# Low parts of weight sums by accumulating transfers in place of VectorE subtractions

## The chip, the cores and the metric

The kernel runs on one core of a Trainium2 chip. The core has a matrix engine (TensorE, PE in the profile), VectorE (DVE), ScalarE (ACT), GpSimd (POOL) and SyncE (SP), each with its own queue of instructions that it works off in order, and 16 DMA engines that all queues share. TensorE writes to PSUM banks; the others work on SBUF tiles of 128 partitions. The metric is the device time of one execution in microseconds.

## The reference, cut to what matters

The reference is one layer of a hybrid block on 256 tokens of width 2048: a gated delta rule branch and a sparse attention branch, merged and projected, then a layer norm, a gated feed-forward part of hidden width 5632, and a second layer norm. All of it is float32. What matters here is the first half of the feed-forward part:

```python
h_gate, h_up = jnp.split(x @ w_ffn_in[l], 2, axis=-1)
x = layer_norm(DEEPNORM_ALPHA * x + (jax.nn.silu(h_gate) * h_up) @ w_ffn_out[l], ln2_g[l], ln2_b[l])
```

## The kernel before

**Split numbers.** TensorE multiplies in a rounded form of float32 (fp32r). To keep precision, each operand is split into a high part (the rounded value, by a ScalarE copy) and a low part (the value minus the high part, by a VectorE subtraction), and a product is three matmuls: high by high, low by high, high by low (`mm3`, L217 to L219). `split(hi, lo, src)` at L207 to L209 is one such copy and one such subtraction.

**Chunks.** Weights stream in chunks of 128 partitions by 1024 numbers (512 KB). `chunk` (L84 to L94) issues the load on SyncE's queue into one of four `raw` tiles, the copy to `hi` on ScalarE (L91) and the subtraction to `lo` on VectorE (L93).

**Groups.** The first feed-forward product runs as a first block, `wfi`, in two parts, and then ten groups (`x_group`, i = 1 to 10), each with 1024 columns of `wfg` and eight pairs of chunks. Some pairs of a group take seven products in place of eight, by Strassen's scheme (`seven_pair`): they need sums of the weight tiles (t1 to t4), split into high and low parts, beside forms of the activations (`f_form`). Their partial results go to four PSUM banks that are read by `sums_chain` (L1065 to L1072). Each group takes four banks (`aux` or `acc`) for its result and four of the other kind for these partial results, and the kinds swap from group to group, so a group's first matmuls write banks that `sums_chain` of the group before must have read. Group 1 runs pairs 0 to 7 in order, with seven products in pairs 4 and 6. Groups 2 and 3 run pairs 1, 3, 2, 0, 4, 5, 6, 7, with seven products in 0, 2, 4 and 6.

**Ready sums.** In most pairs the sums are made in `seven_pair` itself. For pair 0 of groups 2 and 3 (`NEAR`) they are made ahead, in `f_forms_chain`, while group 1 runs, and kept in `near` tiles. `near[0]` is one pair of raw tiles that serves both groups one after the other; `near[1]` and `near[2]` hold the high and low parts for group 2, `near[3]` and `near[4]` those for group 3. For each group the chain issues two loads (L1390, SyncE), makes four sums in place in the raw tiles (`four_sums`, VectorE, L934, L935, L938, L939) and splits the two tiles (L208 on ScalarE, L209 on VectorE).

**Order.** The program is written as a main line with side chains. The main line calls `tick()` after each half pair; `yield n` in a chain means "go on n ticks later". TensorE's and SyncE's queues hold their instructions in the order in which the code issues them (`manual_schedule`). The order on ScalarE, VectorE and GpSimd is made by a planner that goes by readiness in its own model and by priority; loads and splits of chunks have a priority some 70 instructions ahead of their place. Counted from the start of group 1 (16 ticks per group), the chain's loads for group 2 stand at ticks 3 and 4, the sums at 6 and 7, the splits at 8 and 9; the loads for group 3 at 13 and 14, the sums at 16 and 17, the splits at 18 and 19. `sums_of` then hands the tiles to `seven_pair` (L269), which reads them as t1 to t4 in the fourth pair of groups 2 and 3.

**GpSimd's queue** in this stretch holds stores of hidden rows to memory (`put_out`, L1250) and of their forms (L1462).

Of the kernel before, what the change touches and what calls it, by code (L numbers as in the profile page):

```python
# [8 lines left out]
F32 = mybir.dt.float32  # L9
F32R = mybir.dt.float32r  # L10
U32 = mybir.dt.uint32
AF = mybir.ActivationFunctionType
OP = mybir.AluOpType
# [50 lines left out]
def block_kernel(ctx: ExitStack, tc: tile.TileContext, xT, x, cpack, onehot, relb, convw, alog, dtb, gnw,  # L64
                 ws, wws, win, wz, wgt, wba, wbb, woa, wob, wfi, wfg, wfo, ln1g, ln1b, ln2g, ln2b, out):
    nc = tc.nc
# [17 lines left out]
    def chunk(src, pool=None, lead=LEAD):  # L84
        n = src.shape[1]
        pool = pool or wp
        with tc.high_priority(offset=lead):
            raw = wp.tile([P, n], F32, name="raw", tag="raw")
            nc.sync.dma_start(raw, src)
            hi = pool.tile([P, n], F32R, name="hi", tag="hi")  # L90
            nc.scalar.copy(hi, raw)  # L91
            lo = pool.tile([P, n], F32R, name="lo", tag="lo")
            nc.vector.tensor_sub(lo, raw, hi.bitcast(F32))  # L93
        return hi, lo  # L94
# [112 lines left out]
    def split(hi, lo, src):  # L207
        nc.scalar.copy(hi, src)  # L208
        nc.vector.tensor_sub(lo, src, hi.bitcast(F32))  # L209
# [225 lines left out]
    for i in range(8):  # L435
        k0 = 2 * i
        parts = [srcs[i]] if i > 2 else [srcs[i][:, :512], srcs[i][:, 512:]]
        for j, src in enumerate(parts):
# [9 lines left out]
            else:  # L448
                split(*xp, xr)
                hi, lo = chunk(src, lead=0)  # L450
# [479 lines left out]
    def four_sums(ra, rb, lead=0):  # L930

        r0, r1, s0, s1 = (t[:, n * 512:n * 512 + 512] for t in (ra, rb) for n in range(2))
        with tc.high_priority(offset=lead):
            nc.vector.tensor_add(r0, r0, s1)  # L934
            nc.vector.tensor_add(s1, r1, s1)  # L935
        yield 1
        with tc.high_priority(offset=lead):
            nc.vector.tensor_add(r1, r0, r1)  # L938
            nc.vector.tensor_add(s0, r1, s0)  # L939
# [113 lines left out]
    def x_form(q, dst, x32, g):  # L1053
        x32 = x32.rearrange("p (k t) -> p k t", k=2)
        g = g.rearrange("p (i t) -> p i t", i=4)
        ks = slice(2 * q % 4, 2 * q % 4 + 2)
        nc.vector.tensor_add(x32, XH[q // 2][:, ks].bitcast(F32), XL[q // 2][:, ks].bitcast(F32))
        forms([g[:, j] for j in range(4)], x32[:, 0, :P], x32[:, 0, P:], x32[:, 1, :P], x32[:, 1, P:])
        split(*dst, g)
# [192 lines left out]
    def fetch(i, j):  # L1252
# [4 lines left out]
    near = [[hp_.tile([P, 1024], F32R if i > 1 else F32, name="near", tag=f"{hl}{i}") for hl in ("hH", "hL")]  # L1257
            for i in range(1, 5)]
# [74 lines left out]
    def fv():  # L1333
        return fp.tile([P, 512], F32, name="v", tag="v", bufs=4)
# [41 lines left out]
    def f_forms_chain():  # L1376
        yield "x1"
        for tb in range(NTB):
            yield 2
            nc.sync.dma_start(d_x1[tb], x1[tb])  # L1380
        t = [rp.tile([P, 2, 2, 4, P], F32R, name="f_form", tag=f"x1_{tb}") for tb in range(NTB)]
        for i, q in enumerate((4, 6, 2, 0)):
            yield 1
            f_form[q] = t[i // 2][:, i % 2, 0], t[i // 2][:, i % 2, 1]
            x_form(q, f_form[q], fv(), fv())
        yield 1
        raw = near[0]
        for m, g in enumerate(NEAR):
            for i in range(2):
                nc.sync.dma_start(raw[i], wfg[g - 1, i])  # L1390
                yield 1
            yield 1
            yield from four_sums(*raw)
            for i in range(2):
                yield 1
                split(near[1 + 2 * m][i], near[2 + 2 * m][i], raw[i])
            k_ready[g][0] = sums_of(near[1 + 2 * m], near[2 + 2 * m])
            yield 4

    k_ready = {g: {} for g in KEPT + NEAR}  # L1400

    def sums_of(hi, lo):
        (t1, t2), (t4, t3) = ([(hi[i][:, n * 512:n * 512 + 512], lo[i][:, n * 512:n * 512 + 512]) for n in range(2)]
                              for i in range(2))
        return t1, t2, t3, t4

    def kept_load(m):
# [8 lines left out]
        k_ready[KEPT[m]][0] = sums_of(*zip(*kept))  # L1416

    start(f_forms_chain())
    for tb, ps in enumerate(block_xs([wfi[1, k] for k in range(8)], xh, xl)):
        start(h_chain(1, tb, gated(tb, ps), ps_acc))  # L1420
# [325 lines left out]
```

## Time and profile before

| | |
|---|---|
| median of 3 runs | 1456.29 us (1454.67 to 1456.54) |
| the profiled execution's own time | 1454.49 us |
| its span, first to last instruction | 1452.7 us |
| granted TensorE clock | 0.999 |
| group 1's matmuls | about 794 to 836 us of the span |

All times in profile rows count from the start of the span. A row of a timeline gives the start, the duration in us, the engine, the line, the operation with output and input tiles, and in brackets the idle time of the engine just before with what ended it. A row of busy time by stage gives the stretch and its length, then the busy us and the number of instructions of TensorE, its weight loads, VectorE, ScalarE and GpSimd, then the granted clock, the busy share of the 16 DMA engines and GB/s. A row of a tile's view gives the least, median and greatest duration in ns and the first and last start; its last line gives the time from a transfer's issue to its landing. A row of a queue gives packets, MB and its share of the 16 engines' time.

### The profile page before, as it was taken

How to read it: one execution, taken by the hardware profiler on the slowest of the kernel's cores; microseconds unless marked ns; L12 is line 12 of the kernel's file. 1: busy time of each engine (PE TensorE's matmuls, PEld its weight loads, DVE VectorE, ACT ScalarE, POOL GpSimd, SP SyncE). 2: the span in 40 equal slices, each digit the busy share in tenths (PEclk: the TensorE clock that was granted, in tenths of full speed). 3: DMA queues.
4: the chain of work that ended last, by engine and by line, in shares of the span. 5: the costliest groups of instructions: out<-in, count | busy, mean ns of one | idle time of the engine just before them, and what ended most of it. 6: DMA issues, size and time to landing. Idle time of an engine off the chain costs nothing.

```text
span 1452.7 us, 19640 instructions
## 1 busy us (share of the span) xinstructions
PE 1443.7 (99%) x7140; PEld 1213.8 (84%) x7140; DVE 1279.0 (88%) x1763; ACT 813.9 (56%) x1021; POOL 56.2 (4%) x75
## 2 busy tenths in 40 slices
PE   9999999999999999999999999999999999999998
PEld 8888888888888888888888878888888888888887
DVE  6798988789699959998886999989999998989987
ACT  5765454557456646655435665656566565554552
POOL 0002011121000000000000000000000000000000
PEclk9999999999999999999999999999999999999999
DMA  8646589854556755756856767777766666887863
GB/s 293 197 159 196 175 216 335 295 187 151 169 198 232 233 193 198 247 188 204 304 202 218 264 236 253 251 271 255 279 211 212 216 215 247 311 342 265 315 215 118
DMA packets 101969, 336.40 MB, mean 232 GB/s; under 512 B 17696, under 2 KB 18888, under 8 KB 101360
## 3 DMA queue, kind: packets, MB, share of 16 engines
q1 hardware_dynamic: 88512, 310.03, 62.0%
q0 software_dynamic: 6176, 22.75, 4.6%
q10 hardware_dynamic: 7184, 2.36, 0.7%
q8 instruction: 56, 0.92, 0.2%
q14 instruction: 41, 0.34, 0.1%
HBM read 312.88 MB, written 22.22 MB: 231 GB/s over the span
## 4 chain that ended last, share of the span: by engine, by line
PE 92%; DVE 3%; DMA 3%; issue 1%; ACT 1%; SPq 0%; POOLq 0%; DVEq 0%; ACTq 0%
PE acc L217 10%; PE acc L218 10%; PE acc L219 10%; PE acc L153 10%; PE aux L218 9%; PE aux L217 9%; PE aux L219 9%; PE acc L156 5%; PE acc L175 3%; PE acc L173 3%; PE acc L174 3%; PE aux L173 2%; PE aux L174 1%; PE aux L175 1%; DMA raw<-in_win_dram 1%; PE aux L737 1%
## 5 line engine op out<-in xcount | busy, mean ns | idle before, releaser
L91 ACT CAST hi<-raw 128x1024 fp32r<-128x1024 f32 (+1 forms) x388 | 396.9, 1032 | 345.3 <-PE acc L219 87.3
L93 DVE TENSOR_TENSOR lo<-raw,hi 128x1024 fp32r<-128x1024 f32 (+1 forms) x388 | 463.5, 1205 | 87.3 <-ACT hi L91 84.7
L153 PE MATMUL acc<-X,hi 128*128 128x512 f32 x640 | 203.7, 400 | 0.0
L217 PE MATMUL acc<-hi,X 128*128 128x512 f32 x369 | 145.0, 393 | 0.8 <-DVE v L1072 0.8
L156 PEld LDWEIGHTS acc<-X,lo 128*128 128x128 f32 x640 | 120.2, 188 | 28.3
L219 PE MATMUL acc<-hi,X 128*128 128x512 f32 x369 | 143.7, 389 | 0.0
L218 PE MATMUL acc<-lo,X 128*128 128x512 f32 x369 | 143.6, 389 | 0.0
L156 PE MATMUL acc<-X,lo 128*128 128x256 f32 x640 | 126.0, 278 | 0.0
L217 PE MATMUL aux<-hi,X 128*128 128x512 f32 x313 | 122.4, 391 | 0.0
L219 PE MATMUL aux<-hi,X 128*128 128x512 f32 x313 | 121.9, 389 | 0.0
L218 PE MATMUL aux<-lo,X 128*128 128x512 f32 x313 | 121.8, 389 | 0.0
L153 PEld LDWEIGHTS acc<-X,hi 128*128 128x128 f32 x640 | 97.5, 189 | 2.0 <-ACT hi L91 0.7
L241 ACT CAST f_thi<-f_wt 128x1024 fp32r<-128x1024 f32 x58 | 61.0, 1053 | 46.4 <-DVE f_wt L251 23.9
L217 PEld LDWEIGHTS acc<-hi,X 128*128 128x128 f32 x369 | 69.3, 188 | 15.9 <-DVE v L1072 1.2
L219 PEld LDWEIGHTS acc<-hi,X 128*128 128x128 f32 x369 | 69.3, 188 | 14.5
L218 PEld LDWEIGHTS acc<-lo,X 128*128 128x128 f32 x369 | 69.3, 188 | 13.9
L242 DVE TENSOR_TENSOR f_tlo<-f_wt,f_thi 128x1024 fp32r<-128x1024 f32 x58 | 70.6, 1220 | 6.2 <-ACT f_thi L241 6.1
L219 PEld LDWEIGHTS aux<-hi,X 128*128 128x128 f32 x313 | 58.8, 188 | 12.3
L218 PEld LDWEIGHTS aux<-lo,X 128*128 128x128 f32 x313 | 58.8, 188 | 12.1
L217 PEld LDWEIGHTS aux<-hi,X 128*128 128x128 f32 x313 | 58.8, 188 | 12.0
L241 ACT CAST thi<-wt 128x1024 fp32r<-128x1024 f32 x36 | 37.9, 1054 | 49.0 <-DVE wt L246 31.6
L173 PE MATMUL acc<-hi,X 128*128 128x512 f32 x160 | 64.3, 402 | 0.0
(681 smaller groups left out, 3123.6 us busy)
## 6 DMA issues: line engine op xcount, KB each, us to landing
raw<-in_wfg_dram SPq DMA_DIRECT2D x125, 512.0 KB, 4.8
raw<-in_wws_dram SPq DMA_DIRECT2D x80, 512.0 KB, 4.1
raw<-in_wfo_dram SPq DMA_DIRECT2D x70, 512.0 KB, 5.0
raw<-in_wgt_dram SPq DMA_DIRECT2D x49, 512.0 KB, 3.9
f_wraw<-in_wfg_dram SPq DMA_DIRECT2D x29, 512.0 KB, 6.2
raw<-in_win_dram SPq DMA_DIRECT2D x21, 512.0 KB, 4.1
wraw<-in_wfo_dram SPq DMA_DIRECT2D x18, 512.0 KB, 5.1
gt<-d_g SPq DMA_DIRECT2D x18, 512.0 KB, 6.8
```

Of the source, the lines that this page charges most:

```text
L91: nc.scalar.copy(hi, raw)
L93: nc.vector.tensor_sub(lo, raw, hi.bitcast(F32))
L153: nc.tensor.matmul(pss[c], hv[:, kk, cs[c]], X2[k // 4][:, k % 4], start=(k == 0), stop=False, skip_group_check=True)
L156: nc.tensor.matmul(pss[c][:, :S], lv[:, kk, cs[c]], xh[:, k, :], start=False, stop=(k == KT - 1), skip_group_check=True)
L173: nc.tensor.matmul(ps, xh, hv[:, kk], start=(k == 0), stop=False)
L174: nc.tensor.matmul(ps, xh, lv[:, kk], start=False, stop=False)
L175: nc.tensor.matmul(ps, xl, hv[:, kk], start=False, stop=(k == 2 * n - 1))
L217: nc.tensor.matmul(o, sh, hi, start=first, stop=False)
L218: nc.tensor.matmul(o, sh, lo, start=False, stop=False)
L219: nc.tensor.matmul(o, sl, hi, start=False, stop=last)
L241: nc.scalar.copy(hi, v)
L242: nc.vector.tensor_sub(lo, v, hi.bitcast(F32))
```

## The change

For both groups, the two subtractions on VectorE are replaced. ScalarE writes the high part as before and then a copy of it with the sign turned into the low part's tile. GpSimd's queue then issues a transfer from the raw tile to the low part's tile that adds what it carries to what stands there, so that the tile ends as raw minus high. The wait of the chain behind a group's set grows from 4 to 8 ticks, so the loads for group 3 stand at ticks 17 and 18, its sums at 20 and 21 and its splits at 22 and 23.

```diff
@@ -1393,9 +1393,12 @@
             yield from four_sums(*raw)
             for i in range(2):
                 yield 1
-                split(near[1 + 2 * m][i], near[2 + 2 * m][i], raw[i])
+                hi, lo = near[1 + 2 * m][i], near[2 + 2 * m][i]
+                nc.scalar.copy(hi, raw[i])
+                nc.scalar.activation(lo, hi.bitcast(F32), AF.Copy, scale=-1.0)
+                nc.gpsimd.dma_start(lo, raw[i], accum_op=OP.add)
             k_ready[g][0] = sums_of(near[1 + 2 * m], near[2 + 2 * m])
-            yield 4
+            yield 8
```

## The prediction

> **What bounds the kernel now.** I read the page first, then the busy time by stage, then TensorE's own timeline where the change lies.
>
> ```profile
> span 1452.7 us, 19640 instructions
> ...
> PE 1443.7 (99%) x7140; PEld 1213.8 (84%) x7140; DVE 1279.0 (88%) x1763; ACT 813.9 (56%) x1021; POOL 56.2 (4%) x75
> ```
> ```profile
> 0.00:40.00 40.00, 36.81 (x274) 35.46 (x275) 25.99 (x43) 24.12 (x38) 2.11 (x8) 1.00 0.86 288
> 40.00:1410.00 1370.00, 1368.84 (x6684) 1147.39 (x6683) 1220.25 (x1676) 778.66 (x970) 52.21 (x65) 1.00 0.68 233
> 1410.00:1452.00 42.00, 38.09 (x186) 30.95 (x184) 32.79 (x47) 11.09 (x14) 1.85 (x2) 0.96 0.39 134
> ```
> TensorE is the bound. Between 40 and 1410 us it idles 1370.00 - 1368.84 = 1.16 us at full clock; the rest of its idle time is at the two ends, which the change does not touch. Work taken off VectorE is worth only what TensorE waits for it. The timeline shows where that is, the border from feed-forward group 1 to group 2:
>
> ```profile
> 837.07 0.39 PE L219 MATMUL acc<-hi,X 128*128 128x512 f32 x1
> 837.47 0.50 PE L217 MATMUL acc<-hi,X 128*128 128x512 f32 x1
> 837.81 0.39 PE L218 MATMUL acc<-lo,X 128*128 128x512 f32 x1
> 838.04 0.40 PE L219 MATMUL acc<-hi,X 128*128 128x512 f32 x1
> 839.21 0.50 PE L217 MATMUL acc<-hi,X 128*128 128x512 f32 x1 [0.78 <-DVE v L1072]
> 839.54 0.39 PE L218 MATMUL acc<-lo,X 128*128 128x512 f32 x1
> ```
> Matmuls start 0.23 us apart when nothing is late (837.81 to 838.04). Here 837.07 to 837.47 takes 0.40, 837.47 to 837.81 takes 0.34, 838.04 to 839.21 takes 1.17 and 839.21 to 839.54 takes 0.33. Over 0.23 each, that is 0.17 + 0.11 + 0.94 + 0.10 = 1.32 us lost, because VectorE's reads of group 1's shared banks (L1072 and the step before it) come late. This is all that the change can win.
>
> **The change, part by part.**
>
> Removed: four subtractions on VectorE.
>
> ```profile
> L1390 SPq DMA_DIRECT2D near<-in_wfg_dram x4: 424/426/426, 785.4 to 810.1; - x4
> L208 ACT CAST near<-near x4: 1049/1054/1057, 797.0 to 831.2; 128x1024 fp32r<-128x1024 f32 x4
> L209 DVE TENSOR_TENSOR near<-near x4: 1219/1220/1221, 801.3 to 834.4; 128x1024 fp32r<-128x1024 f32 x4
> ...
> L217 PE MATMUL aux<-near,f_form x3: 389/389/389, 855.9 to 857.2; 128*128 128x512 f32 x3
> ...
> L217 PE MATMUL acc<-near,f_form x3: 389/389/389, 897.6 to 899.0; 128*128 128x512 f32 x3
> ...
> DMA to landing us min/median/max: 6.6/7.1/8.0
> ```
> ```profile
> 793.46 0.69 DVE L934 TENSOR_TENSOR near<-near 128x512 f32<-128x512 f32 x1 [3.08 <-DMA near<-in_wfg_dram]
> ...
> 803.75 1.22 DVE L209 TENSOR_TENSOR near<-near 128x1024 fp32r<-128x1024 f32 x1
> 804.88 1.22 DVE L93 TENSOR_TENSOR lo<-raw,hi 128x1024 fp32r<-128x1024 f32 x1
> ...
> 824.34 0.69 DVE L934 TENSOR_TENSOR near<-near 128x512 f32<-128x512 f32 x1
> ...
> 832.67 1.22 DVE L209 TENSOR_TENSOR near<-near 128x1024 fp32r<-128x1024 f32 x1
> 833.81 0.68 DVE L1067 TENSOR_TENSOR v<-v,acc 128x512 f32<-128x512 f32 x1
> ...
> 838.47 0.68 DVE L1072 TENSOR_TENSOR v<-acc,v 128x512 f32<-128x512 f32 x1
> ```
> One shows 1.22 us but holds the engine 804.88 - 803.75 = 1.13, so 4 x 1.13 = 4.5 us goes, all of it ahead of L1072 in VectorE's order. VectorE is solid there:
>
> ```profile
> 795.00:800.00 5.00, 5.00 (x24) 4.14 (x23) 4.97 (x9) 2.35 (x3) 0.00 (x0) 1.00 0.51 151
> 800.00:805.00 5.00, 5.00 (x26) 4.14 (x25) 5.00 (x9) 3.83 (x7) 0.00 (x0) 1.00 0.80 286
> 805.00:810.00 5.00, 5.00 (x24) 4.14 (x23) 5.00 (x11) 2.09 (x4) 0.58 (x1) 1.00 0.87 306
> 810.00:815.00 5.00, 5.00 (x24) 4.14 (x23) 5.00 (x7) 2.52 (x4) 0.55 (x1) 1.00 1.02 335
> 815.00:820.00 5.00, 5.00 (x24) 4.14 (x23) 5.00 (x5) 4.80 (x6) 0.00 (x0) 1.00 0.89 333
> 820.00:825.00 5.00, 5.00 (x24) 4.14 (x23) 5.00 (x7) 0.79 (x2) 0.00 (x0) 1.00 0.49 168
> ```
> Moved: the second set (for group 3) starts four ticks later. In order of the code its loads go from ticks 13 and 14 (in group 1) to 17 and 18, behind the loads of group 2's first pair; its four additions go from ticks 16 and 17 to 20 and 21, past the border. They are 0.69 us each at most, so up to 2.8 us more leaves the queue ahead of L1072 if the planner keeps that order. Together 4.5 to 7.3 us is freed where 1.3 is missing. The gain ends at 1.3: L1067 waits for the ScalarE copy of a bank that starts at 830.69, and four steps of 0.68 behind its end at 831.27 put L1072's end at 834.0 at best, against 837.3, when TensorE would first miss them.
>
> ```profile
> L1066 ACT COPY v<-acc x1: 579/579/579, 830.7 to 830.7; 128x512 f32<-128x512 f32 x1
> ```
> Added on ScalarE: four scaled copies of 128x1024. Before has no such form; the nearest rows are the cast (1.05) and an activation of the same size:
>
> ```profile
> L571 ACT ACTIVATE s_mn<-s_mn 128x1024 f32<-128x1024 f32 x2 | 2.1, 1063 | 0.1
> ```
> I take 1.06, so 4.2 us in all. The first two fall between 797 and 802, where ScalarE is free 10.00 - 2.35 - 3.83 = 3.8 us of 10 and needs 2.1: nothing. Without that cover the next casts would be 2.1 us late, and the low part behind them too.
>
> Added on GpSimd's queue: four accumulating transfers of 512 KB. No accumulating transfer is in this trace. The nearest are GpSimd's stores of the same size:
>
> ```profile
> L1250 POOL DMA_DIRECT2D d_h<-pass x6: 533/533/582, 805.3 to 894.5; - x6
> ...
> DMA to landing us min/median/max: 4.8/6.9/8.2
> ```
> ```profile
> q1 hardware_dynamic: 2775, 10.05, 67.0%
> q0 software_dynamic: 288, 1.05, 6.2%
> ```
> The second view covers 795 to 840: GpSimd's two stores took 6.2% of 45 us for 1.05 MB, 1.4 us of all 16 engines each; a load takes 0.67 x 45 / 10.05 x 0.524 = 1.6. An accumulating one reads two tiles and writes one. Lower bound: like a store, 4.8 us to landing. Upper bound: the rows give none; four times the longest, 33 us, is where I stop. I take twice the median, 14 us and 2.8 us of the engines, since the destination is read as well. The issue itself is 0.53 to 0.58 us; a store of group 1's first hidden rows may go out that much later, and its reload comes only past 1200 us.
>
> What waits for them: group 2 uses the first set at 855.9 and group 3 the second at 897.6, 40 us and more behind, so the low parts themselves are not late. The new wait is elsewhere. Both sets share one raw tile pair, and the reload of it on SyncE's queue must now wait for the accumulating transfer's landing instead of for a subtraction that ended by 805. SyncE's queue is in order of the code; the reload comes right behind this load:
>
> ```profile
> 824.48 0.33 SPq L89 DMA_DIRECT2D raw<-in_wfg_dram  x1
> ```
> The first set's casts started at 797.0 and 799.7; with 1.05 for each of two ScalarE steps and 0.6 for the issue, the second accumulating transfer starts at about 802.4. At 14 us it lands at 816, 8 us before SyncE comes by (6 if VectorE's relief brings SyncE there sooner). No wait: nothing.
>
> In the 16 engines' time: two accumulating transfers (5.6 us) come between 799 and 817, and the second set's two loads (3.2 us) leave it, for 825 and later; the share at 820 to 825 is 0.49. Net 2.4 us more in a stretch, 800 to 820, that has 5 x (0.20 + 0.13 + 0 + 0.11) = 2.2 us free of 20. Loads land up to that much later; TensorE's margins are of the same size:
>
> ```profile
> 814.51 2.43 DVE L242 TENSOR_TENSOR f_tlo<-f_wt,f_thi 128x1024 fp32r<-128x1024 f32 x2
> ...
> 816.85 1.22 DVE L93 TENSOR_TENSOR lo<-raw,hi 128x1024 fp32r<-128x1024 f32 x1
> ```
> ```profile
> 820.30 0.39 PE L217 MATMUL aux<-hi,X 128*128 128x512 f32 x1
> ```
> This low part is ready at 818.07 and used 0.23 behind 820.30: 2.4 us. VectorE's own relief by then (two subtractions, 2.3 us) pays for the delay: nothing.
>
> [...]
>
> **Sum.** -1.3 (border) + 0 (ScalarE) + 0 (queue) + 0 (engines) = -1.3 us. The span becomes 1451.4 and the profiled execution's 1454.49 becomes 1453.2; this execution lies 1.8 under the median of 1456.29, so the median becomes 1455.0.
>
> **The rivals.**
>
> 1. The border's gap stays. VectorE is in order too: if the planner puts the moved additions ahead of L1067, they wait for loads issued at about 825 that take 7.1 to 8.0 us, so until 832 to 834; two to four additions and four steps of 0.68 then end L1072 at 836 to 839.5, against 839.15 now. For it: at 793.46 VectorE idled 3.08 us for such a load. Against: the four ticks' delay. It gives 1455.0 to 1456.5, say 1456.3.
>
> 2. Slower: the accumulating transfer is long. If it lands more than 24 us after its issue at 802.4, the reload holds SyncE's queue past 826; with 7.1 to land, the additions then hold VectorE past 833.4, and with 2.4 for them and 2.7 for the four steps L1072 ends past the 838.3 that TensorE needs. Queued behind are the loads of the next pair and the low parts of every later chunk. From that point each microsecond is one of TensorE; at 33 us it is 33 - 24 - 1.3 = 8 lost, 1464. For it: nothing bounds this kind of transfer. Against: it needs over three times the store's median of 6.9.
>
> 3. Contention: at four times a store's engine time (5.6 us each), two take 11.2, less the 3.2 that leave and the 2.2 free, 5.8 us of delay; minus the margin of 2.4 and the relief of 2.3 that is a stall of 1.1, 1456; at six times (8.4 each), 6.7, 1462. For it: the share of 0.87 to 1.02 at 805 to 815. Against: the half-idle engines at 820 to 825 take the overhang.
>
> 4. Nothing moves: the planner fills VectorE's freed time so that L1072 keeps its place. It gives 1456.3.
>
> **How the numbers follow.** Forecast 0.55, rivals 1 and 4 together 0.27, rival 2 0.09, rival 3 0.07 (half of it slower by over 0.2%), and 0.02 for a gain beyond the 1.3 us that the rows allow. 0.2% is 2.9 us, about what a measurement of this kernel can tell from no change. Forecast and rivals 1 and 4 lie inside it. Slower: 0.09 + 0.035, about 0.13. Faster by over 2.9 us is more than TensorE's idle time in the whole middle; with a run's own spread of 1.9 us (1454.67 to 1456.54) I give it 0.04. Same 0.83. The range goes from 1453.0 (the forecast less the spread) to 1459.0 (rival 3, the small form of rival 2).
>
> **What would show it.** Right: no gap at L217 after L1072, TensorE's middle idle time near zero, no SyncE wait on a transfer before the second reload, VectorE's busy time down by about 4.9 us (4 x 1.22), ScalarE's up by 4.2. Wrong: a landing of over 20 us for the accumulating transfers, a SyncE wait near 825 with VectorE idle behind it, or a TensorE gap between 815 and 850 that was not there.

## The result and the profile after

The changed kernel takes 1463.98 us (median of 6 runs, 1461.27 to 1467.38) against 1456.22 us of the kernel before beside it: 1.0061 times as long, 95% interval 1.0050 to 1.0071. It is slower by 0.61%, some 8.9 us by the ratio (the two medians lie 7.8 us apart), where 1455.0 was forecast. The profiled execution took 1462.91 us. Of the runs below, two single executions far from all others (3756.07 us with the second set only, 1798.49 us with plain copies) stand outside the ratios.

The page of the changed kernel, span and engines:

```profile
span 1461.1 us, 19653 instructions
...
PE 1446.2 (99%) x7140; PEld 1214.0 (83%) x7140; DVE 1275.6 (87%) x1759; ACT 818.0 (56%) x1025; POOL 59.7 (4%) x79
...
q0 software_dynamic: 6752, 24.85, 5.3%
```

Busy time by stage, first the kernel after, then the kernel before (stretch and length; busy us of TensorE, weight loads, VectorE, ScalarE, GpSimd; granted clock, DMA share, GB/s):

```profile
40.00:795.00 755.00, 753.72 (x3935) 638.58 (x3934) 643.65 (x1003) 416.06 (x543) 39.94 (x42) 1.00 0.65 215
795.00:900.00 105.00, 98.73 (x436) 79.12 (x436) 92.22 (x117) 63.78 (x79) 6.88 (x10) 1.00 0.73 240
900.00:1410.00 510.00, 510.00 (x2283) 422.69 (x2282) 474.60 (x547) 298.73 (x349) 8.97 (x17) 1.00 0.73 260
```
```profile
40.00:795.00 755.00, 754.63 (x3936) 638.86 (x3935) 642.28 (x1001) 416.18 (x544) 39.96 (x42) 1.00 0.64 214
795.00:900.00 105.00, 104.21 (x469) 85.83 (x468) 104.55 (x135) 64.59 (x80) 4.32 (x8) 1.00 0.72 244
```

Most of the loss is in one stretch, 795 to 900 us: TensorE idles 105.00 - 98.73 = 6.27 us there against 0.79 before, and starts 33 matmuls fewer. VectorE, which had less to do, was busy 92.22 us in place of 104.55: it waited. Between 900 and 1410 nothing is lost. TensorE's timeline of the kernel after names each stall (start, duration, operation; in brackets the idle time just before and what ended it):

```profile
819.99 0.39 PE L217 MATMUL acc<-f_thi,f_form 128*128 128x512 f32 x1
821.08 0.50 PE L218 MATMUL acc<-f_tlo,f_form 128*128 128x512 f32 x1 [0.70 <-DVE f_tlo L242]
822.34 0.40 PE L217 MATMUL aux<-hi,X 128*128 128x512 f32 x1
823.42 0.50 PE L218 MATMUL aux<-lo,X 128*128 128x512 f32 x1 [0.68 <-DVE lo L93]
...
836.25 0.39 PE L217 MATMUL aux<-hi,X 128*128 128x512 f32 x1
837.49 0.50 PE L218 MATMUL aux<-lo,X 128*128 128x512 f32 x1 [0.86 <-DVE lo L93]
...
841.25 0.39 PE L219 MATMUL acc<-hi,X 128*128 128x512 f32 x1
842.76 0.49 PE L217 MATMUL acc<-hi,X 128*128 128x512 f32 x1 [1.12 <-DVE v L1071]
843.33 0.40 PE L219 MATMUL acc<-hi,X 128*128 128x512 f32 x1
843.97 0.49 PE L217 MATMUL acc<-hi,X 128*128 128x512 f32 x1 [0.24 <-DVE v L1072]
...
865.96 0.39 PE L217 MATMUL aux<-f_thi,f_form 128*128 128x512 f32 x1
868.27 0.50 PE L218 MATMUL aux<-f_tlo,f_form 128*128 128x512 f32 x1 [1.92 <-DVE f_tlo L242]
...
869.53 0.39 PE L217 MATMUL aux<-f_thi,f_form 128*128 128x512 f32 x1
870.54 0.50 PE L218 MATMUL aux<-f_tlo,f_form 128*128 128x512 f32 x1 [0.62 <-DVE f_tlo L242]
```

From start to start, over the 0.23 us of undisturbed matmuls, about 1.9 us go at 820 to 824, 3.0 us at 836 to 844 and 3.1 us at 865 to 871: 8.0 us, less the 1.3 us that the kernel before lost at its border, 6.7 us of the 8.4 by which the spans differ (1461.1 - 1452.7). About 1 us more of the difference is there before 778 us, ahead of the changed work: the group's first load goes out that much later.

VectorE's timeline of the kernel after shows what those operands waited for:

```profile
818.67 1.23 DVE L246 TENSOR_TENSOR f_wt<-f_wraw,raw 128x1024 f32<-128x1024 f32 x1 [4.88 <-DMA raw<-in_wfg_dram]
819.81 2.42 DVE L242 TENSOR_TENSOR f_tlo<-f_wt,f_thi 128x1024 fp32r<-128x1024 f32 x2
822.15 1.22 DVE L93 TENSOR_TENSOR lo<-raw,hi 128x1024 fp32r<-128x1024 f32 x1
...
835.61 0.69 DVE L934 TENSOR_TENSOR near<-near 128x512 f32<-128x512 f32 x1 [5.90 <-DMA near<-in_wfg_dram]
836.22 3.49 DVE L93 TENSOR_TENSOR lo<-raw,hi 128x1024 fp32r<-128x1024 f32 x3
839.63 0.68 DVE L1067 TENSOR_TENSOR v<-v,acc 128x512 f32<-128x512 f32 x1
...
843.23 0.69 DVE L1072 TENSOR_TENSOR v<-acc,v 128x512 f32<-128x512 f32 x1
```

And the chain of waits of the kernel after, its two longest transfers (start, us, what):

```profile
809.73 8.85 DMA raw<-in_wfg_dram
...
828.33 7.19 DMA near<-in_wfg_dram
```

Two waits of VectorE carry this. **At 828 to 835** the first moved addition (L934) stands ahead of three chunks' low parts (L93) and of L1067. It waits 5.90 us for its load, which SyncE issued at 827.85. The three low parts were wanted by TensorE from 836.48 on and were made from 836.22 to 839.7 one behind the other; L1067 to L1072 come behind them, and L1072 starts at 843.23 in place of 838.47. VectorE then runs solid, behind by what it lost, and at 866 to 871 the low parts of sums (`f_tlo`, L242) are late once more. **At 813 to 818** a sum for a seven-product pair (L246) now stands ahead of three low parts (L242 twice, L93) and waits 4.88 us for a chunk's load; before, VectorE was solid here and TensorE lost nothing.

The lines are not in the order that they had before. VectorE's order around the border, by line number (T is L242 on `f_tlo`):

```
before  ... 251 T T 93 246 93 242 242 250 T 251 934 935 T 93 938 939 93 93 93 209 1067 209 1068 1428 1071 93 1072
after   ... 246 93 250 T 242 251 242 246 T T 93 250 93 251 242 242 T 93 934 93 93 93 1067 935 1068 938 1071 939 1072 93
```

### The profile page after: what moved, and what is told of

Its sections match the earlier page's. It is cut to its first block, busy times and chain, and to the rows that moved or that the text cites. A ratio compares the mean times of both kernels' runs of the same rounds, so it can differ in the third digit from the quotient of the medians.

```text
span 1461.1 us, 19653 instructions
## 1 busy us (share of the span) xinstructions
PE 1446.2 (99%) x7140; PEld 1214.0 (83%) x7140; DVE 1275.6 (87%) x1759; ACT 818.0 (56%) x1025; POOL 59.7 (4%) x79
## 3 DMA queue, kind: packets, MB, share of 16 engines
q0 software_dynamic: 6752, 24.85, 5.3%
## 4 chain that ended last, share of the span: by engine, by line
PE 90%; DMA 4%; DVE 4%; issue 1%; ACT 1%; SPq 0%; POOLq 0%; DVEq 0%; ACTq 0%
PE acc L219 10%; PE acc L218 10%; PE acc L217 10%; PE acc L153 10%; PE aux L218 9%; PE aux L219 9%; PE aux L217 9%; PE acc L156 5%; PE acc L175 3%; PE acc L173 3%; PE acc L174 3%; PE aux L175 1%; PE aux L173 1%; PE aux L174 1%; DVE lo L93 1%; PE aux L737 1%
## 5 line engine op out<-in xcount | busy, mean ns | idle before, releaser
L93 DVE TENSOR_TENSOR lo<-raw,hi 128x1024 fp32r<-128x1024 f32 (+1 forms) x388 | 464.6, 1209 | 89.2 <-ACT hi L91 86.6
L242 DVE TENSOR_TENSOR f_tlo<-f_wt,f_thi 128x1024 fp32r<-128x1024 f32 x58 | 70.8, 1223 | 7.1 <-ACT f_thi L241 7.0
```

What stands on the lines that cost most here:

```text
L242: nc.vector.tensor_sub(lo, v, hi.bitcast(F32))
```

## The experiments

Ratios are to the kernel before, run beside each on the same chip, with 95% intervals. The times in the expectations go from 1456.2 us for the kernel before; beside these runs it took 1454.4 to 1454.9 us, so the ratios are what to compare. Line numbers are those of the changed kernel; in the move alone, the transfers alone and the subtractions with the longer wait the subtractions stay.

**The move alone.** The additions go four ticks later, the subtractions stay.

```diff
-            yield 4
+            yield 8
```

> Only the longer wait of the chain (8 ticks for 4); the four subtractions stay on VectorE, no accumulating transfer. The planner puts the moved additions between the four steps of group 1's partial sums, the first of them behind L1067. Theory A (VectorE's new order costs the time, where instructions that wait for late loads stand ahead of ready ones): the additions come behind L1067 here and the order up to the border is that of before, so little is lost, 1455 to 1458. Theory B (the engine time of the accumulating transfers costs it): 1456, no change. Theory C (the move by itself costs it, since the additions wait for loads issued at 825): VectorE idles 3 to 6 us near 835 and the time is 1459 to 1462.

Measured: 1.0007 (0.9997 to 1.0016). Theory C is out; A and B both fit this run. VectorE's timeline of this kernel:

```profile
831.92 0.68 DVE L1067 TENSOR_TENSOR v<-v,acc 128x512 f32<-128x512 f32 x1
832.52 0.68 DVE L934 TENSOR_TENSOR near<-near 128x512 f32<-128x512 f32 x1
...
835.52 0.68 DVE L1072 TENSOR_TENSOR v<-acc,v 128x512 f32<-128x512 f32 x1
```

Busy time by stage:

```profile
825.00:850.00 25.00, 25.00 (x117) 20.77 (x116) 23.75 (x30) 16.07 (x21) 0.00 (x0) 1.00 0.64 228
850.00:875.00 25.00, 23.64 (x102) 18.72 (x101) 25.00 (x29) 15.51 (x19) 2.12 (x4) 1.00 0.77 258
```

With the subtractions in place the planner puts the same late addition behind L1067 and behind the low parts, and it waits for nothing. L1072 is even 3 us earlier than before, and TensorE is busy all of 825 to 850: the border's gap is gone, and 1.4 us are lost at 850 to 875 instead. So the tick count alone is not the cause; the order that the planner gives is.

**The transfers alone.** The subtractions stay and do all the work; an accumulating transfer of the same size follows each. VectorE's order is that of the kernel before, instruction for instruction.

```diff
                 split(near[1 + 2 * m][i], near[2 + 2 * m][i], raw[i])
+                nc.gpsimd.dma_start(raw[i], near[2 + 2 * m][i].bitcast(F32), accum_op=OP.add)
```

> The kernel before, with its subtractions and its wait of 4 ticks, and four accumulating transfers of 512 KB added, each from the finished low part onto the raw tile (which is reloaded or dead afterwards). VectorE's order is that of before, instruction by instruction. The reload at 809.6 must now wait for the transfer. Theory A (order): the transfers lengthen landings at 800 to 820 but the old order has nothing waiting there, 1456 to 1458. Theory B (transfers): the loads of the pairs after the reload are late, TensorE stalls near 820 and 836, 1460 to 1464.

Measured: 1.0019 (1.0009 to 1.0028), 2.8 us. The transfers cost something by themselves, about a third of the loss, more than theory A had and less than theory B. Where, its profile doesn't fully show: the profiled execution took 1455.13 us, one of three short ones among ten (the other seven lie between 1457.8 and 1460.0). It does show a delay that the changed kernel has not: without the move SyncE comes by early, and the second of its two reloads, which must wait for the transfers, starts at 813.4 in place of 810.1 in the kernel before. So these 2.8 us need not be the same loss as that of the transfers in the changed kernel.

**The order alone.** The changed kernel without its transfers.

```diff
-                nc.gpsimd.dma_start(lo, raw[i], accum_op=OP.add)
```

> The changed kernel without the accumulating transfers: the low parts of the sums of groups 2 and 3 hold minus the high part, so the output differs. VectorE's order is that of the changed kernel up to 862 us. Theory A (order): the stalls at 820, 836 to 843 and 866 stay, 1461 to 1464. Theory B (transfers): loads land in 4 to 5 us again and the stalls go, 1455 to 1457. If both are needed: the stall at 820 goes (its load then lands before VectorE arrives), that at 836 stays, 1458 to 1461.

Measured, on four executions: 1.0040 (1.0025 to 1.0055), 5.8 us, as theory A had it. VectorE's timeline:

```profile
818.02 1.23 DVE L246 TENSOR_TENSOR f_wt<-f_wraw,raw 128x1024 f32<-128x1024 f32 x1 [2.71 <-DMA raw<-in_wfg_dram]
...
834.51 0.69 DVE L934 TENSOR_TENSOR near<-near 128x512 f32<-128x512 f32 x1 [5.44 <-DMA near<-in_wfg_dram]
835.12 3.49 DVE L93 TENSOR_TENSOR lo<-raw,hi 128x1024 fp32r<-128x1024 f32 x3
```

The wait at the border is there with no accumulating transfer in the program, 5.44 us in place of 5.90. The wait at 818 is 2.71 us in place of 4.88.

**No move.** The changed kernel with the old wait of 4 ticks.

```diff
-            yield 8
+            yield 4
```

> The changed kernel with the old wait of 4 ticks. The four additions of the second set stand together ahead of four low parts and of L1067; the reload waits for the first set's transfers (landing near 811). Theory A (order): the stall at 820 stays (2 us), the additions wait less than now because their loads go out near 811 and land near 818, so the border loses little: 1457 to 1460. Theory B (transfers): as in the changed kernel, 1462 to 1465. Theory C (the move): without the move no idle VectorE at 830 to 835, 1456 to 1458.

Measured: 1.0016 (1.0006 to 1.0025), as theory A had it. The second set's loads are early again and the border holds. The wait at 820 is there, and longer on TensorE in the profiled execution, which at 1460.13 us is the longest of its ten (median 1457.03); its timeline and busy time by stage:

```profile
820.08 0.39 PE L217 MATMUL acc<-f_thi,f_form 128*128 128x512 f32 x1
823.39 0.79 PE L218 MATMUL acc<-f_tlo,f_form 128*128 128x512 f32 x1 [2.92 <-DVE f_tlo L242]
823.98 0.63 PE L219 MATMUL acc<-f_thi,f_form 128*128 128x512 f32 x1
824.40 0.63 PE L217 MATMUL aux<-f_thi,X 128*128 128x512 f32 x1
```
```profile
823.00:826.00 3.00, 2.61 (x6) 2.10 (x7) 3.00 (x4) 3.00 (x4) 0.00 (x0) 0.55 0.03 11
```

After the pause the matmuls from 823.98 to 826.54 are 0.43 us apart in place of 0.23; the granted clock of the stretch is 0.55. Here too SyncE comes by early: its two reloads at 812.44, which must wait for the transfers, take 3.15 us to issue in place of 0.90 in the changed kernel. The move that cost 6 us at the border is also what kept the reload clear of the transfers in the changed kernel.

**A longer wait.** 12 ticks in place of 8, and the same without the transfers. VectorE's order is the same in both; L934 stands some 40 places behind L1067.

```diff
-            yield 8
+            yield 12
```

> The changed kernel with a wait of 12 ticks, which takes the second set's additions from ahead of three low parts and L1067 to far behind the border (L934 stands 40 places behind L1067). The order around 820 is that of the changed kernel. Order theory: the 5.9 us idle of VectorE at 830 to 835 and TensorE's stalls at 836 to 843 go, those at 820 to 823 (2 us) stay: 1457 to 1460. If the stalls near 866 hang on the border, they go too. Transfer theory: the same four transfers run, so the time stays at 1462 to 1464.

> The one before without its four accumulating transfers (the low parts of the sums of groups 2 and 3 hold minus the high part, so the output differs). VectorE's order is the same, instruction by instruction, so the difference of the two is the transfers alone. If the transfers matter only through late loads that VectorE's order waits for: 1455.5 to 1457, with a stall of about 1 us left at 821 as in the run of the order alone, and 1 to 3 us below the one before. If the transfers cost nothing: equal to the one before.

Measured: 1.0014 (1.0003 to 1.0024) with the transfers, 0.9996 (0.9988 to 1.0005) without; as the order theory had it, and the transfer theory's 1462 to 1464 is out. Busy time by stage with them, then without them:

```profile
795.00:900.00 105.00, 104.00 (x468) 85.62 (x467) 98.59 (x128) 68.94 (x85) 7.94 (x12) 1.00 0.78 261
```
```profile
795.00:900.00 105.00, 104.79 (x473) 86.59 (x472) 101.17 (x132) 69.75 (x85) 4.31 (x8) 1.00 0.71 246
```

With the moved additions out of the way the stalls at 836 to 844 and at 866 to 871 are both gone, with the transfers and without. That the later one is the backlog of the first fits this, and a VectorE busy 24.86 of 25 us at 850 to 875 in the changed kernel; it was not tried by itself. With the order-alone run the four make a square:

| | with the transfers | without |
|---|---|---|
| wait of 8 ticks | 1.0061 | 1.0040 |
| wait of 12 ticks | 1.0014 | 0.9996 |

Down the columns the place of the additions is worth 0.0047 and 0.0044 of 1455 us, 6.8 and 6.4 us, with intervals far apart. Along the rows the transfers are worth 0.0021 and 0.0018, 3.1 and 2.6 us, beside 2.8 where they stood alone. The two add up. Within a row the intervals overlap a little, and the medians of the two runs at 12 ticks differ by 1.7 us, so the size of the transfers' part is less sure than that of the place: 1.7 to 3.1 us. That they cost something at all is borne out by the transfers alone, whose interval lies above 1.

**Second set only.** The first set is split by VectorE as before, the second by transfers, with a wait of 12.

```diff
+                if not m:
+                    split(near[1 + 2 * m][i], near[2 + 2 * m][i], raw[i])
+                    continue
...
-            yield 8
+            yield 12
```

> The first set is split by VectorE's subtractions as before, the second by accumulating transfers, with a wait of 12 ticks. VectorE's order is that of before past 820, and nothing of the second set stands ahead of the border. Order theory: no stall at 820, none at 836 to 843, the border's 1.3 us are won, and two transfers in a later stretch cost 0 to 1: 1453.5 to 1455.5. Transfer theory: half of the loss, 1458 to 1460.

Measured: 0.9992 (0.9983 to 1.0001), median 1453.56 us. Its busy time by stage:

```profile
795.00:900.00 105.00, 105.00 (x475) 87.10 (x474) 103.42 (x134) 68.16 (x84) 6.13 (x10) 1.00 0.77 258
```

TensorE has no idle time left in the stretch. This is what the forecast wanted, and it's the best of the versions, but its interval includes no change. It doesn't say which of two things at 800 to 820 costs time, since with the first set's subtractions back both are gone: its transfers, and L246's place ahead of the low parts (VectorE waits for no chunk's load there).

**Subtractions with the longer wait.** The kernel before with 12 ticks.

```diff
-            yield 4
+            yield 12
```

> The kernel before with a wait of 12 ticks in place of 4 and nothing else: subtractions on VectorE, no transfers. The additions and subtractions of the second set (7 us of VectorE) leave the queue ahead of the border. If the border's gap is 1.3 us of waiting for VectorE as the prediction has it, 1453.5 to 1454; if another instruction is late next, 1454.5 to 1456.

Measured: 1.0008 (0.9999 to 1.0016). Its busy time by stage:

```profile
825.00:850.00 25.00, 25.00 (x116) 20.76 (x115) 23.44 (x28) 16.26 (x21) 0.01 (x1) 1.00 0.69 245
...
875.00:900.00 25.00, 24.00 (x109) 19.40 (x108) 25.00 (x32) 14.61 (x20) 1.06 (x2) 1.00 0.69 234
```

The border's gap is gone here too, and a stall of 1.0 us comes at 875 to 900. With the subtractions kept, the longer wait passes the lack of VectorE time on: the second expectation came. (By their rows, the four additions and two subtractions are 4 x 0.69 + 2 x 1.22 = 5.2 us, not 7.)

**Plain copies.** The wait of 12 ticks, with transfers that only write.

```diff
-                nc.gpsimd.dma_start(lo, raw[i], accum_op=OP.add)
+                nc.gpsimd.dma_start(lo.bitcast(F32), raw[i])
```

> The kernel with the wait of 12 ticks (1456.1), with its four accumulating transfers replaced by plain copies of the same 512 KB from the raw tile to the low part's tile (the low parts hold the unsplit sums, so the output differs). VectorE's order is the same. If accumulating is what costs (the destination is read too): the issue falls from 0.89 to about 0.55 us, the engine time from 2.65 to 1.4 us each, and the time lies between 1454.5 and 1455.5. If any four transfers of 512 KB at that place cost as much: 1456.

Measured: 0.9995 (0.9986 to 1.0005), as without any transfer, which points at the accumulating as what costs. The profile doesn't show the gain: its execution, at 1456.68 us the longest of the ten in the ratio, still has TensorE idle 0.94 us at 795 to 900, against 1.00 with accumulating transfers. GpSimd's transfers on the page (packets, MB, share of 16 engines over the span), plain copies, then accumulating ones with the same wait, then none:

```profile
q0 software_dynamic: 6752, 24.85, 4.8%
```
```profile
q0 software_dynamic: 6752, 24.85, 5.2%
```
```profile
q0 software_dynamic: 6176, 22.75, 4.5%
```

Spans are 1454.9, 1453.4 and 1452.0 us, so the three come to 69.8, 75.6 and 65.3 us: four plain copies took 4.5 us of all engines, 1.1 each, and four accumulating ones 10.3, 2.6 each. The same bytes, over twice the time (the shares are rounded to 0.1%, so each figure is good to some 0.4 us).

**Double transfers.** The wait of 12 ticks, and behind each accumulating transfer a second one.

```diff
                 nc.gpsimd.dma_start(lo, raw[i], accum_op=OP.add)
+                nc.gpsimd.dma_start(raw[i], lo.bitcast(F32), accum_op=OP.add)
```

> The kernel with the wait of 12 ticks, with a second accumulating transfer behind each (back onto the raw tile, which is dead or reloaded afterwards). VectorE's order is the same. If the transfers cost by their engine time in the busy stretch at 800 to 820: the loss against none doubles, from about 1.7 to 2.6 now to 3.5 to 5, 1457.5 to 1460, with a longer stall at 820. If only the first one meets the load that VectorE waits for: 1456 to 1457.

Measured: 1.0015 (1.0006 to 1.0024), against 1.0014 with one each. The median, 1457.00 us, is the upper edge of the second expectation, and the two intervals leave room for 2 us more or less. The page has 6.0% of 1457.0 us on this queue, 87.4 us, so eight took 22.1 us, 2.8 each. Busy time by stage of the profiled execution, at 1458.79 us the longest of its eleven:

```profile
795.00:900.00 105.00, 102.08 (x460) 84.03 (x459) 96.74 (x122) 67.57 (x82) 10.88 (x15) 1.00 0.85 265
```

TensorE idles 2.9 us here, where with one transfer each it idled 1.0. So twice the engine time did not clearly cost more, and whether only the transfers that run while VectorE waits for the load at 818 matter is not shown.

## Why the prediction was wrong

**What held.** TensorE's waits are what counts, and the border's 1.3 us can be won: with the second set only, nothing of it is left. ScalarE's busy time rose by 818.0 - 813.9 = 4.1 us (4.2 forecast), and with its added copies but no transfers and the wait of 12 the kernel is no slower (0.9996): they cost nothing. The engines' time, taken as twice a store's, was 2.8 us per transfer; from 5.3% of 1461.1 less 4.6% of 1452.7 it is 2.65. The reason given for it, that the destination is read as well, no view shows: the queue's bytes are the same for plain copies (24.85 MB). VectorE lost 3.4 us (1279.0 to 1275.6), neither the 4.9 of the forecast's sign nor the 4.5 of its own working, four times 1.13; where the rest went is open.

**Rival 2 gave the right number for a wrong reason.** It needed a landing of over 24 us. Transfers at 798 to 818 in the kernel after (kind, number, KB, median us to landing), and the loads in the same window of the kernel before:

```profile
raw<-in_wfg_dram SPq DMA_DIRECT2D x5, 512.0 KB, 6.4
...
near<-near POOLq DMA_DIRECT2D x2, 512.0 KB, 7.6
```
```profile
raw<-in_wfg_dram SPq DMA_DIRECT2D x6, 512.0 KB, 4.2
```

They landed in 7.6 us, half of the 14 taken, and SyncE had no wait on one in the kernel after. That 1464 came out is chance.

Nor did the transfers' issue wait for a pause of VectorE: the row of the kernel after shows an accumulating transfer's issue (0.89 us) and the start of a store's, 1.17 us of GpSimd together, beside a VectorE busy 4.93 of 5.00:

```profile
800.00:805.00 5.00, 5.00 (x25) 4.14 (x24) 4.93 (x10) 4.92 (x8) 1.17 (x2) 1.00 1.03 276
```

**The step that failed first: rival 1's price, and its chance.** The mechanism was named: the moved additions, placed ahead of L1067, wait for loads that go out at about 825. It happened, with loads at 827.85 and 7.19 us to landing: the term -1.3 (border) took the additions to be "past the border", "if the planner keeps that order", and the planner put the first of them ahead of L1067, so that L1072 ended at 843.9 in place of 834.0. But the price, 1455.0 to 1456.5, counted only L1072. The three low parts between the waiting addition and L1067 were not listed, though the prediction said of rival 2 that "the low parts of every later chunk" queue behind such a wait. Nor was the backlog: an engine that is busy 104.55 of 105 us before can't make up 5.90 us, and seems to hand it on to 866 us. The square prices this at 6.4 to 6.8 us, where the sum had -1.3. With it rival 1 would have read about 1462, and its share of the 0.27 would have stood on the slower side.

**The step that failed second: "VectorE's own relief by then (two subtractions, 2.3 us) pays for the delay: nothing."** The freed time was not there at 816 to 820. The planner spent it by drawing L246 forward, ahead of the three low parts that TensorE wants from 820 on, and L246 needs a load. That loads set VectorE's pace there, with four raw tiles, and that a solid busy row hid it, fits the rows; no run had more tiles. The wait is 2.71 and 2.35 us without the transfers, 4.88 and 4.32 with them (8 and 12 ticks): the longer landing falls on that load. It took 8.85 us in the kernel after; over the chunks' loads of 798 to 818 the median to landing was 6.4 us there, and with the wait of 12 it was 6.5 with the transfers and 4.2 without. The forecast of 2.4 us net for the engines was about right in size; the cover was not. This term is 2.6 to 3.1 us by the ratios in place of 0.

**What stays open.** Why the planner's model sets L934 ahead of L1067 once the subtractions are gone, and behind it while they stand, isn't known; that it does is shown by the orders. Of the transfers' 2.6 us with the wait of 12, the profiled executions show 0.8 as TensorE's idle time at 795 to 900. Two of the eleven executions with the transfers took 1460.2 and 1460.5 us, where none without them took over 1456.0; neither has a trace, so what was late in them is open.

## What to carry to other kernels

Where a planner orders an engine, an instruction taken away can change the order of all that stands near it (here L934 came ahead of L1067): read the new order, or treat it as an unknown with a price, before a saving is counted. A wait on an engine that works in order holds up what is queued behind it (here 5.90 us on VectorE, and L1072 at 843.23 in place of 838.47), so list those instructions by their due times, and give a moved consumer its load's issue and landing (here 827.85 and 7.19 us) before its place. An engine that is busy all the time may still be paced by its loads (VectorE was busy 5.00 of 5.00 us at 815 to 820, and in the kernel after it waited 4.88 us for one there); time freed there may be worth nothing until the load is earlier.

## What the runs showed of the hardware

- An accumulating transfer of 512 KB between tiles took 2.6 us of the 16 engines with the wait of 12, 2.65 in the kernel after and 2.8 with double transfers, a plain copy between the same tiles 1.1. Its issue held GpSimd 0.89 us (877 to 932 ns in the kernel after), the plain copy's 0.54 (532 to 573 ns).
- TensorE's clock fell to about half after one pause of 2.92 us (3.31 from start to start, without the move): 0.55 at 823 to 826. A pause of 2.23 us, in the run with double transfers, kept 1.00 (820 to 825), and so did the one of 1.92 us at 866 in the kernel after:

```profile
866.00:870.00 4.00, 2.00 (x8) 1.05 (x6) 4.00 (x5) 2.85 (x4) 0.09 (x1) 1.00 0.96 308
```

What sets the clock, and how long a pause it takes, no run shows beyond these three.
